# Weights of plain blocks and output units: hi and lo split in two parts of 1024 columns instead of four of 512

## The chip, the cores and the metric

The kernel runs on one core of one Trainium2 chip. The metric is device time in microseconds (us) for one call, the median of the runs. Engines are named as in the profile: PE (matrix multiply), DVE (vector), ACT (scalar), POOL (the third elementwise engine), SP (the queue that issues the transfers).

## The reference

One step of a hybrid layer on 512 new prompt tokens and 8 sequences of 8 sample tokens, all float32, D_MODEL 2048. The layer normalises x, projects it, runs a gated linear attention branch (GLA, 4 heads) and a gated delta branch (GDN, 16 heads, with a causal convolution of width 4 on q, k and v), projects both, merges them through sigmoid gates and projects once more. Cut to its core:

```python
h = _rmsnorm(x, ln_g)
proj = h @ w_in
o_a, s_gla_new = _gla_chunked(q_a, k_a, v_a, log_alpha, s_gla)
y_a = (_rmsnorm(o_a, gla_norm_g) * silu(gate_a)) @ w_br_a
qkv, conv_new = _causal_conv(qkv_b, conv_buf, conv_w)
o_b, s_gdn_new = _gdn_chunked(q_b, k_b, v_b, g, beta, s_gdn)
y_b = (_rmsnorm(o_b, gdn_norm_g) * silu(gate_b)) @ w_br_b
out = x + (sigmoid(m_a) * y_a + sigmoid(m_b) * y_b) @ w_out
```

The result is the final norm of `out` and the new states of both branches and of the convolution, for prompt and sample.

## The kernel before

The 576 tokens (512 prompt, 64 sample) are the moving side of nearly all matrix products. A **block** is 128 columns of a weight matrix, all 2048 rows deep: in SBUF a tile of 128 partitions by 16 k-steps by 128 columns, 2048 elements in a partition. `load_raw` (one SP transfer of 1024 KB) brings it in as `raw`. `split` makes two tiles from it: `hi`, the weights cast to fp32r, on ACT (line 249, ACT CAST hi), and `lo = raw - hi`, on DVE (line 252; on POOL for the blocks 0 and 2). Each k-step of `run_half` then issues three products, hi by the first and the second part of the tokens and lo by the first, for 256 tokens (half 0) and again for 320 (half 1). `raw`, `hi` and `lo` have two buffers each, so block i+1 is split while block i is multiplied.

`split` has four parts (`NSPL`), each a quarter of the columns: 512 elements a partition. Part j of block i+1 is written in `run_half` of block i, two in each half (after k-steps 1 and 9). The same holds, with other counters, for the output units (`run_unit`) and for the last group before them. The two branch projections (`run_pairs`) have their own `pairs_prep`, which casts and subtracts in pieces of 1024 already (lines 383 and 384); `split` only calls it.

Beside the blocks run many **side tasks**, written as generators (`key_task`, `query_task`, `value_task`, `vtask`, `gla_chain`, `solve` and others). `S.pump`, called after each k-step, resumes those whose due time has come; the clock `S.t` counts the estimated time of PE instructions alone. PE's order is fixed by that: `manual_schedule` holds for PE. ACT, DVE, POOL and SP are put in order by the framework's scheduler, from the order of writing and its own estimates. Each engine runs its row strictly in order.

Names that come up below:

- GLA values: `vT<-mm` (line 1274) copies each half of a value block from PSUM on ACT; then `vtask` transposes it on PE (`vtp`, line 125) and casts it (`vth`, line 1229). There are 4 such blocks in each of 4 heads.
- GDN queries and values: ACT scales (`acc`, line 859), DVE adds three taps of the convolution (`acc`, line 861); per chunk of a head DVE computes `z` (line 1428), PE multiplies `np_<-z,U`, DVE copies `nn` (line 1434), PE multiplies `spd<-nn,ke`.
- `conv_rows` (line 872): PE transposes `lp`, DVE copies it out as `ls` (line 879), PE transposes `lpp` into the same ring of three PSUM buffers. `vh`, `vhs` and `U` are DVE copies of the next head's values and of its solved triangle (lines 1406, 1408, 1349).
- Decay of GLA: DVE adds a bias to `lg` and gets `ab` (line 798), a chain over four rows j on DVE and POOL (`scb` and `ab`, lines 813 to 818) ends in one transfer `d_c<-ab` a row (line 821). The second group of four rows reuses the tile `ab`, so its first `ab` waits for the last `d_c`.
- `key_task`: SP loads `R<-d_gh` (line 941, one buffer), POOL adds a mask to it (lines 943 and 945), ACT makes `W` from it (lines 948 and 950).

Of the kernel before, what the change touches and what calls it, by code (L numbers as in the profile page):

```python
# [103 lines left out]
def build(ctx, tc, nc, x_p, x_s, st_gla, st_gdn, st_conv, ln_g, w_in, w_al, b_al, conv_w,  # L104
# [76 lines left out]
    blocks = []  # L181
# [33 lines left out]
            SY.dma_start(raw, b["wd"][:, c0:c0 + P].rearrange("(k p) c -> p k c", p=P))  # L215
        wts[i] = [raw, None, None]

    NSPL = 4

    NM0, NMP, NMG, NMD, NM1 = 5, 0, 3, 3, 12  # L220

    def split(i, j, eng=V):

        if i >= len(blocks):
            return
        if blocks[i]["wd"] is None:
            if j in (1, 3):
                pairs_prep(blocks[i], j // 2)  # L230
            return
        w = wts[i]
        narrow = blocks[i]["col"] is None
        if i == len(blocks) - 1:
            if j == 0:
                w[1:] = (ost["pr"].tile([P, KT, P], F32R, name=n) for n in ("hi_", "lo_"))
        elif j == 0 and narrow:
            w[1] = p0c.tile([P, KT, 112], F32R, name="hin")
            G.memset(w[1][:, :, 48:64].bitcast(F32), 0.0)
        elif j == 0:  # L240
            w[1] = wp.tile([P, KT, P], F32R, name="hi", tag="whi")
            w[2] = wp.tile([P, KT, P], F32R, name="lo", tag="wlo")
        raw, hi, lo = w
        s = slice(j * KT // NSPL, (j + 1) * KT // NSPL)
        if narrow:
            raw, hi, lo = raw[:, s], hi[:, s, 0:48], hi[:, s, 64:112]
        else:
            raw, hi, lo = raw[:, s], hi[:, s], lo[:, s]
        hc = A.copy(hi, raw)  # L249
        if i > 2:  # L250
            S.marks[A] = hc
        cut = eng.tensor_tensor(out=lo, in0=raw, in1=hi.bitcast(F32), op=ALU.subtract)  # L252
        if eng is V:
            last_split[0] = cut
# [3 lines left out]
    def run_half(i, hf, ps):  # L258
        b = blocks[i]
        rh, rl = b["rhs"]  # L260
        narrow = b["col"] is None
        m = 112 if narrow else P
        _, hi, lo = wts[i]
        t0, t1 = HALVES[hf]
        out = ps[0:m, 0:t1 - t0]
        for k in range(KT):
            r1, r2 = rh(k)[:, t0:t1], rl(k)[:, t0:t1]
            mm(out, hi[:, k, 0:m], r1, start=(k == 0), stop=False)
            mm(out, hi[:, k, 0:m], r2, start=False, stop=(narrow and k == KT - 1))
            if not narrow:  # L270
                mm(out, lo[:, k, 0:m], r1, start=False, stop=(k == KT - 1))
            if i >= 3 and k % 8 == 1:
                split(i + 1, hf * 2 + k // 8)
            elif i == 2 and hf == 1 and k % 4 == 1:
                split(3, k // 4)
            S.pump()
        b["evac"](hf, out, slice(t0, t1))

# [118 lines left out]
    def run_pairs(i):  # L397
        b = blocks[i]
        cols = b["pairs"]
        n = len(cols)  # L400
        t1, t2 = slice(0, TH), slice(TH, T)
        for p in range(n):
# [3 lines left out]
            for j in range(7):  # L406
                g = 7 * p + j
# [12 lines left out]
                for kk in range(KH):  # L420
# [4 lines left out]
                    if kk == 1:  # L425
# [9 lines left out]
                            pairs_raw(b, p + 1, 0)  # L435
                        elif j == 3:
                            pairs_raw(b, p + 1, 1)
                    if g == 7 * n - 1 and kk % 2 == 0:
                        if kk == 0:
                            pr_.pop(("hi", 0)), pr_.pop(("lo", 0))  # L440
                        split(i + 1, kk // 2)
                    S.pump()
                for kk in range(KH):
                    r1, r2 = b["rhs"](j, kk)
# [63 lines left out]
    def run_unit(i):  # L508

        b = blocks[i]  # L510
        g, q = b["col"]
# [5 lines left out]
        end_ = len(blocks) - 1  # L517
# [4 lines left out]
        for n, (u, j, c) in enumerate(order):  # L522
            hi, lo = (x.rearrange("p (j a) c -> p j (a c)", j=4)[:, j] for x in wts[u][1:])
            k = blocks[u]["col"][1] * 4 + j
# [7 lines left out]
            else:  # L532
                both = [(accs[c], m[:, TP:TP + P], hi), (accs[c][0:TS], m[:, T:T + TS], lo)]
                for out, w, x in both[::-1] if last else both:
                    mm(out, w, x, start=(first and x is hi), stop=(last and x is hi))
            if n % 5 == 1 and i < end_ - 1:
                split(i + 1, n // 5)
            if n % 5 == 3 and i == end_ - 2:
                split(i + 2, n // 5)
            S.pump()  # L540
            if last:
                b["evac"](g, c, accs[c])
# [1569 lines left out]
    def third():  # L2112
        for j in range(NSPL):
            split(2, j, G)
# [37 lines left out]
```

## Time and profile before

| what | value |
| --- | --- |
| median of 3 runs | 2812.85 us (2811.58 to 2815.17) |
| profiled execution, its own time | 2812.57 us |
| its span | 2810.9 us |
| PE busy | 2763.3 us, 98% of the span |
| DVE busy | 1804.4 us, 64% |
| ACT busy | 1103.3 us, 39% |
| POOL busy | 364.7 us, 13% |
| mean granted PE clock | 0.994 |

The clock that the throttle grants PE stands at full speed in all 40 slices of the page. PE is idle for 2810.9 - 2763.3 = 47.6 us in all. An engine's time counts for the kernel's time only where PE waits for it, so the list of PE's waits and the slack of its other operands are what to read.

### The profile page before, as it was taken

To read this page: it belongs to the slowest core of one execution; us is meant where nothing else is said; L and a number is where in the kernel's file an instruction comes from. 1 tells how busy PE (TensorE), PEld (TensorE's weight loads), DVE (VectorE), ACT (ScalarE), POOL (GpSimd) and SP (SyncE) were. 2 spreads that over 40 slices of the span, in tenths; PEclk is the share of its full clock that TensorE was granted. 3 is DMA by queue.
4 is the path that set the end of the run, shared out by engine and by line. 5 is a ranking of instruction groups with operands and counts; after the bars stand their busy time and mean duration, and the time that the engine had idled before them with its cause. 6 is when DMAs were issued, how large, how long until landed. Compare 5 with 4: busy or idle time off the path is not lost.

```text
span 2810.9 us, 49996 instructions
## 1 busy us (share of the span) xinstructions
PE 2763.3 (98%) x19726; PEld 2630.9 (94%) x19726; DVE 1804.4 (64%) x3456; ACT 1103.3 (39%) x2449; POOL 364.7 (13%) x545
## 2 busy tenths in 40 slices
PE   8999999999999999999999999999989999999998
PEld 7999999999999999999999999999879889999776
DVE  7767765765567888734666666647754667877333
ACT  5444445565423232223333333336643334434222
POOL 2000000442101010101222222212210010000111
PEclk9999999999999999999999999999999999999999
DMA  5333335565652333435444444457766988657522
GB/s 164 121 120 116 122 118 151 153 182 173 169 128 79 109 96 91 145 90 156 126 122 124 125 120 122 130 146 199 226 220 215 300 285 270 197 175 242 175 76 97
DMA packets 546281, 433.97 MB, mean 154 GB/s; under 512 B 75125, under 2 KB 468293, under 8 KB 544117
## 3 DMA queue, kind: packets, MB, share of 16 engines
q1 hardware_dynamic: 546046, 430.78, 50.7%
q8 instruction: 155, 2.54, 0.4%
q14 instruction: 80, 0.66, 0.1%
HBM read 322.69 MB, written 108.00 MB: 153 GB/s over the span
## 4 chain that ended last, share of the span: by engine, by line
PE 89%; DVE 4%; DMA 1%; ACT 1%; POOL 1%; issue 1%; SPq 0%; DVEq 0%; POOLq 0%; ACTq 0%
PE mm L115 71%; PE oacc L115 7%; PE opd L115 1%; PE sps L115 1%; DVE tmp L906 1%; PE sp L115 1%; DMA raw<-in_w_br_a 1%; PE ksq L115 1%; PE spd L115 1%; PE qk L115 1%; DVE lo L252 0%; PE ksp L115 0%; PE kk L115 0%; DVE nt L909 0%; PE op L125 0%
## 5 line engine op out<-in xcount | busy, mean ns | idle before, releaser
L115 PE MATMUL mm<-hh,hi 128*128 128x256 f32 (+2 forms) x3968 | 1194.6, 304 | 0.0
L115 PE MATMUL mm<-hl,hi 128*128 128x256 f32 (+2 forms) x3968 | 1161.6, 295 | 0.0
L115 PE MATMUL mm<-hh,lo 128*128 128x256 f32 (+2 forms) x3968 | 1117.0, 295 | 0.8 <-DVE lo L252 0.8
L115 PEld LDWEIGHTS mm<-hh,hi 128*128 128x128 f32 x3968 | 748.5, 189 | 10.1 <-issue 4.5
L115 PEld LDWEIGHTS mm<-hl,hi 128*128 128x128 f32 x3968 | 748.9, 189 | 2.1
L115 PEld LDWEIGHTS mm<-hh,lo 128*128 128x128 f32 x3968 | 729.2, 188 | 1.3 <-DVE lo L252 1.0
L252 DVE TENSOR_TENSOR lo<-raw,hi 128x512 fp32r<-128x512 f32 x568 | 398.6, 720 | 315.4 <-ACT hi L249 307.2
L249 ACT CAST hi<-raw 128x512 fp32r<-128x512 f32 x572 | 329.6, 619 | 485.4 <-PE mm L115 407.8
L115 PE MATMUL mm<-lb,hi 128*128 128x320 f32 (+1 forms) x1024 | 208.1, 298 | 0.0
L115 PE MATMUL oacc<-hi,m 128*128 128x512 f32 x540 | 174.1, 395 | 0.0
L115 PEld LDWEIGHTS mm<-lb,hi 128*128 128x128 f32 x1024 | 163.7, 188 | 9.5 <-issue 7.8
L383 ACT CAST hi<-raw 128x1024 fp32r<-128x1024 f32 x96 | 100.9, 1051 | 182.1 <-PE mm L115 105.4
L384 DVE TENSOR_TENSOR lo<-raw,hi 128x1024 fp32r<-128x1024 f32 x96 | 117.3, 1222 | 77.1 <-ACT hi L383 75.3
L115 PE MATMUL mm<-lb,lo 128*128 128x320 f32 (+1 forms) x512 | 150.7, 294 | 0.0
L115 PE MATMUL mm<-tl,hi 128*128 128x288 f32 x512 | 137.7, 295 | 0.0
L115 PE MATMUL mm<-th,hi 128*128 128x288 f32 x512 | 137.6, 296 | 0.0
L906 DVE TENSOR_TENSOR tmp<-nt 128x1 f32<-128x1 f32 (+36 forms) x163 | 131.6, 807 | 3.0
L115 PEld LDWEIGHTS oacc<-hi,m 128*128 128x128 f32 x540 | 101.1, 188 | 28.0 <-DVE mth L462 0.4
L861 DVE SCALAR_TENSOR_TENSOR acc<-ext,cwT,acc 128x600 f32<-128x600 f32 x144 | 120.2, 835 | 0.8 <-ACT acc L859 0.6
L115 PE MATMUL oacc<-lo,m 128*128 128x512 f32 x300 | 118.1, 395 | 0.0
L383 ACT CAST hi<-s 128x1024 fp32r<-128x1024 f32 x72 | 74.8, 1047 | 105.3 <-DVE s L371 50.2
L1449 ACT COPY od<-opd 128x128 f32<-128x128 f32 x64 | 16.8, 262 | 242.2 <-PE opd L115 242.2
(891 smaller groups left out, 3993.1 us busy)
## 6 DMA issues: line engine op xcount, KB each, us to landing
raw<-in_w_in SPq DMA_DIRECT2D x144, 1024.0 KB
raw<-in_w_br_b SPq DMA_DIRECT2D x16, 1024.0 KB
Sb<-in_state_gla SPq DMA_DIRECT2D x32, 512.0 KB
out<-Sb SPq DMA_DIRECT2D x32, 512.0 KB
raw<-in_w_br_a SPq DMA_DIRECT2D x16, 1024.0 KB
raw<-in_w_out SPq DMA_DIRECT2D x16, 1024.0 KB
Sbd<-in_state_gdn SPq DMA_DIRECT2D x16, 512.0 KB
out<-Sbd SPq DMA_DIRECT2D x16, 512.0 KB
```

The costliest lines, as they stand in the source:

```text
L115: PE.matmul(out, lhsT, rhs, start=start, stop=stop, **kw)
L249: hc = A.copy(hi, raw)
L252: cut = eng.tensor_tensor(out=lo, in0=raw, in1=hi.bitcast(F32), op=ALU.subtract)
L383: S.marks[A] = A.copy(hi, src)
L384: last_split[0] = V.tensor_tensor(out=lo, in0=src, in1=hi.bitcast(F32), op=ALU.subtract)
L861: V.scalar_tensor_tensor(out=acc, in0=ext[:, i:i + 600], scalar=cw(i), in1=acc, op0=ALU.mult, op1=ALU.add)
L906: V.tensor_tensor(out=tv, in0=nt[:, cs, c0:i], op=ALU.mult, in1=nt[:, c0:i, i:i + 1].rearrange("p j o -> p o j").broadcast_to([P, m, i - c0]))
L1449: A.copy(o_[:, c], op_[:, 0:P])
```

## The change

`NSPL` is 2: a part is half of the columns, 1024 elements a partition. The calls are thinned out to match: in `run_half` one part in each half, after k-step 1 (it was k-steps 1 and 9), in block 2 both parts in its second half, in the last pair group at kk 0 and 4, in the units at n 1 and 11 (n 3 and 13 for the unit after next). `pairs_prep` is called with j directly, so both its calls come at k-step 1 of a half instead of k-step 9. Computation, tiles, buffers and transfers are the same.

```diff
-    NSPL = 4
+    NSPL = 2
...
         if blocks[i]["wd"] is None:
-            if j in (1, 3):
-                pairs_prep(blocks[i], j // 2)
+            pairs_prep(blocks[i], j)
             return
...
-            if i >= 3 and k % 8 == 1:
-                split(i + 1, hf * 2 + k // 8)
-            elif i == 2 and hf == 1 and k % 4 == 1:
-                split(3, k // 4)
+            if i >= 3 and k == 1:
+                split(i + 1, hf)
+            elif i == 2 and hf == 1 and k % 8 == 1:
+                split(3, k // 8)
...
-                    if g == 7 * n - 1 and kk % 2 == 0:
+                    if g == 7 * n - 1 and kk % 4 == 0:
                         if kk == 0:
                             pr_.pop(("hi", 0)), pr_.pop(("lo", 0))
-                        split(i + 1, kk // 2)
+                        split(i + 1, kk // 4)
...
-            if n % 5 == 1 and i < end_ - 1:
-                split(i + 1, n // 5)
-            if n % 5 == 3 and i == end_ - 2:
-                split(i + 2, n // 5)
+            if n % 10 == 1 and i < end_ - 1:
+                split(i + 1, n // 10)
+            if n % 10 == 3 and i == end_ - 2:
+                split(i + 2, n // 10)
```

PE's row is the same instruction for instruction. DVE's row goes from 2790 to 2566 entries, ACT's from 1643 to 1570, and the scheduler puts the side tasks' instructions in other places among the splits. Line numbers from 230 on are one lower in the changed kernel. Three places follow.

The first is the decay chain of GLA's first group. POOL before, the rows j = 2 and 3 of the chain; `sqk` and `R` belong to two `key_task`s:

```order
L814 COPY scb<-ab 128x4
L815 COPY scb<-ab 128x4
L816 COPY scb<-ab 128x8
L818 TENSOR_TENSOR ab<-ab,scb 128x512
L968 TENSOR_TENSOR sqk<-tb,halfc 128x5
L943 TENSOR_TENSOR R<-R,maskb 128x512
L814 COPY scb<-ab 128x4
L815 COPY scb<-ab 128x4
L816 COPY scb<-ab 128x8
L945 TENSOR_TENSOR R<-R,maskb 128x64
L818 TENSOR_TENSOR ab<-ab,scb 128x512
```

POOL now, at the start of the chain (row j = 0 begins with L813):

```order
L843 MEMSET ext 128x3
L846 COPY ext<-hisk 128x8x3
L942 TENSOR_TENSOR R<-R,maskb 128x512
L944 TENSOR_TENSOR R<-R,maskb 128x64
L813 COPY scb<-ab 128x4
L814 COPY scb<-ab 128x4
L815 COPY scb<-ab 128x8
L817 TENSOR_TENSOR ab<-ab,scb 128x512
```

SP before, the same place; the load of this `R` stands behind two `d_c`:

```order
L821 DMA d_c_105<-ab 128x576
L215 DMA raw<-in_w_in 128x16x128
L821 DMA d_c_106<-ab 128x576
L941 DMA R<-d_gh 128x576
L821 DMA d_c_107<-ab 128x576
L991 DMA d_W_180<-W 128x512
L992 DMA d_W_180<-W 64x64
L821 DMA d_c_108<-ab 128x576
```

SP now:

```order
L990 DMA d_W_180<-W 128x512
L940 DMA R<-d_gh 128x576
L991 DMA d_W_180<-W 64x64
L215 DMA raw<-in_w_in 128x16x128
L820 DMA d_c_105<-ab 128x576
L820 DMA d_c_106<-ab 128x576
```

The two additions to `R` moved from the end of the chain to before its start, and the load of `R` from behind the second `d_c` to behind the preceding head's `W`.

The second place is a value block of GLA, on ACT (`hi` is the next block's first cast). Before:

```order
L1274 COPY vT<-mm 128x256
L249 CAST hi<-raw 128x512
L1274 COPY vT<-mm 128x320
L249 CAST hi<-raw 128x512 x2
L1229 CAST vth<-vtp 128x4x128
```

Now:

```order
L1273 COPY vT<-mm 128x256
L248 CAST hi<-raw 128x1024
L1273 COPY vT<-mm 128x320
L248 CAST hi<-raw 128x1024
L1228 CAST vth<-vtp 128x4x128
```

The order is the same; what stands between the two copies of `vT` is one cast of 1024 instead of one of 512.

The third place is the delta stage, DVE. First the start of a query block, before:

```order
L1465 TENSOR_TENSOR oT<-op_18634,gtd 128x512
L252 TENSOR_TENSOR lo<-raw,hi 128x512
L1428 SCALAR_TENSOR_TENSOR z<-ksp_18675,neghc,vh 128x128
L861 SCALAR_TENSOR_TENSOR acc<-ext,cwT,acc 128x600
L252 TENSOR_TENSOR lo<-raw,hi 128x512
```

Now:

```order
L1464 TENSOR_TENSOR oT<-op_18298,gtd 128x512
L251 TENSOR_TENSOR lo<-raw,hi 128x1024
L860 SCALAR_TENSOR_TENSOR acc<-ext,cwT,acc 128x600
L1427 SCALAR_TENSOR_TENSOR z<-ksp_18339,neghc,vh 128x128
L860 SCALAR_TENSOR_TENSOR acc<-ext,cwT,acc 128x600
```

A tap of the convolution now stands ahead of `z`, and the `lo` ahead of both is the long one; this pattern stands in six heads. Then `conv_rows` at the end of a group of four heads, before:

```order
L886 COPY lp<-lpp 12x128
L1406 TENSOR_SCALAR vh<-vp,sqk 128x128 x3
L879 COPY ls<-lp 96x128
L1406 TENSOR_SCALAR vh<-vp,sqk 128x128
L1408 TENSOR_SCALAR vhs<-vps,sqk 64x128
L1349 TENSOR_SCALAR U_17558<-up 64x4x64
```

Now:

```order
L885 COPY lp<-lpp 12x128
L1405 TENSOR_SCALAR vh<-vp,sqk 128x128 x4
L1407 TENSOR_SCALAR vhs<-vps,sqk 64x128
L1348 TENSOR_SCALAR U_17242<-up 64x4x64
L878 COPY ls<-lp 96x128
```

The second `ls` moved behind the last `vh`, `vhs` and `U`; this stands at three places of the stage.

## Rows read from the trace of the kernel before

**Rows 1.** The page, busy time of each engine over the span.

```profile
PE 2763.3 (98%) x19726; PEld 2630.9 (94%) x19726; DVE 1804.4 (64%) x3456; ACT 1103.3 (39%) x2449; POOL 364.7 (13%) x545
```

**Rows 2.** PE's waits over the whole span: us in total, times, longest.

```profile
PE ksp L125 <- issue: 13.4, 1, 13.4
PE lg L115 <- DVE ab L798: 3.5, 1, 3.5
PE mm L115 <- DVE lo L252: 0.8, 1, 0.8
```

**Rows 3.** The page, costliest groups: busy us, mean ns | idle before, releaser.

```profile
L252 DVE TENSOR_TENSOR lo<-raw,hi 128x512 fp32r<-128x512 f32 x568 | 398.6, 720 | 315.4 <-ACT hi L249 307.2
L249 ACT CAST hi<-raw 128x512 fp32r<-128x512 f32 x572 | 329.6, 619 | 485.4 <-PE mm L115 407.8
...
L383 ACT CAST hi<-raw 128x1024 fp32r<-128x1024 f32 x96 | 100.9, 1051 | 182.1 <-PE mm L115 105.4
L384 DVE TENSOR_TENSOR lo<-raw,hi 128x1024 fp32r<-128x1024 f32 x96 | 117.3, 1222 | 77.1 <-ACT hi L383 75.3
```

**Rows 4.** Timeline, ACT and PE, one value block: start us, us, idle in brackets.

```profile
833.30 0.62 ACT L249 CAST hi<-raw 128x512 fp32r<-128x512 f32 x1 [6.53 <-PE mm L115]
833.83 0.42 ACT L1274 COPY vT<-mm 128x320 f32<-128x320 f32 x1
...
834.32 0.71 PE L125 MATMUL vtp<-ident,vT 128*128 128x128 f32 x5
```

**Rows 5.** Timeline, DVE and PE, `conv_rows` at one of its three places.

```profile
1572.19 0.28 DVE L879 COPY ls<-lp 96x128 f32<-96x128 f32 x1
...
1572.90 0.41 DVE L1349 TENSOR_SCALAR U<-up 64x256 f32<-64x256 f32 x1
...
1572.52 0.28 PE L125 MATMUL lpp<-ident,lvP 128*12 128x128 f32 x1 [0.44 <-DVE ls L879]
```

**Rows 6.** Timeline, ACT, DVE and PE, start of a query block, one of six.

```profile
1646.11 0.63 ACT L249 CAST hi<-raw 128x512 fp32r<-128x512 f32 x1
...
1646.77 0.69 DVE L252 TENSOR_TENSOR lo<-raw,hi 128x512 fp32r<-128x512 f32 x1
1647.38 0.34 DVE L1428 SCALAR_TENSOR_TENSOR z<-ksp,neghc,vh 128x128 f32<-128x128 f32 x1
...
1649.24 0.38 PE L115 MATMUL np__18697<-z,U 128*128 128x128 f32 x2
```

**Rows 7.** Timeline, DVE and PE, another block's start, one of fourteen alike.

```profile
1613.80 0.69 DVE L252 TENSOR_TENSOR lo<-raw,hi 128x512 fp32r<-128x512 f32 x1 [1.56 <-ACT hi L249]
1614.49 0.84 DVE L861 SCALAR_TENSOR_TENSOR acc<-ext,cwT,acc 128x600 f32<-128x600 f32 x1
1615.26 0.35 DVE L1428 SCALAR_TENSOR_TENSOR z<-ksp,neghc,vh 128x128 f32<-128x128 f32 x1
...
1616.55 0.39 PE L115 MATMUL np__18284<-z,U 128*128 128x128 f32 x2
```

**Rows 8.** Timeline, ACT, SP and POOL, the decay chain and the loads of `R`.

```profile
504.73 0.37 SPq L941 DMA_DIRECT2D R<-d_gh  x1
...
508.87 1.28 POOL L943 TENSOR_TENSOR R<-R,maskb 128x512 f32<-128x512 f32 x1 [2.67 <-DMA R<-d_gh]
...
525.82 0.50 POOL L814 COPY scb<-ab 128x4 f32<-128x4 f32 x1 [2.32 <-DVE ab L813]
...
525.87 0.33 ACT L950 ACTIVATE W<-R,nghc 64x64 f32<-64x64 f32 x1
...
543.25 0.32 SPq L821 DMA_DIRECT2D d_c<-ab  x1
```

**Rows 9.** Timeline, POOL, `lo` of block 2 in the startup.

```profile
30.50 3.05 POOL L252 TENSOR_TENSOR lo<-raw,hi 128x512 fp32r<-128x512 f32 x2 [1.91 <-ACT hi L249]
```

**Rows 10.** Timeline, DVE and SP, a raw load of `w_br_a`.

```profile
2396.74 1.29 DVE L252 TENSOR_TENSOR lo<-raw,hi 128x512 fp32r<-128x512 f32 x2
...
2399.17 0.43 SPq L341 DMA_DIRECT2D raw<-in_w_br_a  x1
```

## The prediction

> **What bounds the kernel now.** The page comes first: PE is busy 2763.3 of 2810.9 us, DVE 1804.4, ACT 1103.3 [rows 1]. So PE sets the time, and a shorter cast or subtraction is worth nothing in itself; what counts is where PE waits, 47.6 us in all. The list of PE's waits is read next. It names a `lo` once, for 0.8 us [rows 2]: that is all that the splits cost now. The other large waits have other causes: 13.4 us for a transfer, 3.5 us for the decay chain `ab` [rows 2]. Last come the timelines where a side task's result reaches PE with little to spare, because there a longer split, or one in another place, makes a new wait. I looked for every operand of PE that is ready less than about 1 us before its use, and asked the two orders what now stands ahead of its producer.
>
> **What the split saves, and why it is off the path.** A `lo` of 512 takes 720 ns, one of 1024 takes 1222; a `hi` of 512 takes 619, one of 1024 takes 1051 [rows 3] (the long rows are those of the pair blocks, the same operations on the same tiles). A block needs 4 x 720 = 2880 ns of DVE before and 2 x 1222 = 2444 now, and 2476 against 2102 of ACT. For 568/4 = 142 blocks that is 62 us of DVE and 53 us of ACT. All of it lies beside PE: DVE sits idle for 315.4 us ahead of its `lo`s, waiting for ACT, and ACT for 485.4 us ahead of its `hi`s, mostly waiting for PE to let go of a buffer [rows 3]. Taken as nothing. What it costs: whoever stands behind a part now waits for 1051 ns of ACT or 1222 of DVE instead of 619 or 720.
>
> **GLA value blocks, +3.2 us.** The cast starts when PE frees the buffer, at 833.30; the second copy of `vT` follows it at 833.83, 0.53 later, and ends at 834.25 [rows 4]. PE's five transposes start at 834.32, 0.11 apart; the third is the first that reads the second copy, near 834.54, so the copy has 0.29 to spare [rows 4]. With the long cast the copy starts 1.051 - 0.619 = 0.43 later. A result that PE waits for is used some 0.05 us after it is there (the `ls` of rows 5: ready 1572.47, used 1572.52), so 0.24 is really spare, and PE waits about 0.20. ACT was idle for 6.53 us before [rows 4], so nothing else shifts that. Sixteen blocks (four in each of four heads): 16 x 0.20 = 3.2 us. Bounds: 0, if PE gets there that much later itself, and 16 x 0.43 = 6.9, if nothing is spare. I take 3.2, worked from the block's own rows.
>
> The Trainium skill has a sentence against this change (Perfetto Trace Analysis, Optimizing Scalar/DVE Operations): where these engines are not saturated but make bubbles elsewhere, breaking instructions up may help. The same section says that grouping pays if the engine is saturated. By the second rule the sum would be a gain, at most the 47.6 us that PE stands idle; by the first a loss, as worked out here from the rows. At 64% and 39% busy the trace sides with the first.
>
> **`conv_rows`, +2.5 us.** PE's `lpp` waits for the second `ls` already: ready 1572.47, used 1572.52 [rows 5]. Now `ls` stands behind the fourth `vh`, `vhs` and `U`. The work is the same, only permuted, so `ls` ends when `U` did, at 1572.90 + 0.41 = 1573.31, and `lpp` starts about 0.84 later. Three places: 2.5 us. Behind `lpp` PE has only its own row, nothing there gives the time back. Lower bound 0, if PE comes later itself; upper 3 x 1.2, if a `lo` gets in between.
>
> **`z` in the delta stage, +1.3 us (0 to 6).** At the start of six query blocks `z` follows the first `lo` directly and ends at 1647.72, 1.52 before PE's use at 1649.24 [rows 6]. Now the long cast ends at 1646.11 + 1.05 = 1647.16, 0.39 later than the old `lo` began; the `lo` is 0.50 longer; and a tap of the convolution goes ahead, 0.77 from its start to the next [rows 7]. Together 1.66 against 1.52 - 0.05: PE waits 0.2, six times 1.2 to 1.3. In fourteen other starts the order stays, `lo`, tap, `z`, and `z` ends 0.94 before its use [rows 7]; there the delay is 0.39 + 0.50 = 0.89 against 0.94 - 0.05: it comes out even. That is the thinnest margin of the sum. If each of the twenty lost 0.3, it would be 6. The first head and the copies near it add about 0.4, by the same durations.
>
> **The decay chain, +2.3 us (-1.5 to +4.4).** PE stands 3.5 us for `ab` [rows 2], which waits for the last `d_c`, issued at 543.25 by a chain on POOL that runs from 525.82 without a gap to speak of [rows 8]. Two changes meet there. POOL's two additions to `R` leave the chain: about 1.28 + 0.3 us less [rows 8]. But they now stand ahead of its first operation, and `R` can only be loaded when the last `W` of the preceding head is read. That ended at 526.2 [rows 8]; ACT has some 2 us less ahead of it now (two casts fewer, and `W` goes before the other activations), so about 524. From issue to use the load took 508.87 - 504.73 = 4.14 us [rows 8]. POOL then adds until about 529.7, and the chain starts 3.9 later and is 1.6 shorter: +2.3. If the load came as early as 520 it would be -1.5; if `W` came no earlier than before, +4.4. The four `d_c` themselves are moved past nothing that waits longer than POOL does.
>
> **Startup, +0.7 (0 to 1.6).** POOL subtracts two parts of block 2 in 3.05 us [rows 9]; PE takes the first as soon as it is there. One piece of 1024 is ready some 1.5 us later than one of 512. Two later waits of PE in the startup depend on DVE, not on PE's pace, and take half of it back.
>
> **Block 4, -0.8 us.** The one wait for a `lo` [rows 2] goes: DVE now makes both parts ahead of other work that it had taken first. What is late next there is nothing that the trace shows.
>
> **Raw buffer of `w_br_a`, -1.1 us.** Its load was issued at 2399.17, though the last `lo` had read the buffer at 2398.03 [rows 10]: SP had other transfers ahead. Now it stands first, and later waits of PE for DVE hang on that load. Bounds -1.5 and 0.
>
> **The sum.** 3.2 + 2.5 + 1.3 + 0.4 + 2.3 + 0.7 - 0.8 - 1.1 = +8.5 us. Against the profiled execution's own 2812.57 that is 2821.1; the median lies 0.28 above that execution, so 2821.3.
>
> **The rivals.** *No change that can be measured* (chance 0.27). PE is late by itself at these places, so that one wait swallows the next, and the load of `R` comes early enough. For it: all margins are tenths of a microsecond, and the trace's own rows differ by that. Then the GLA blocks give 1, `conv_rows` 2.5, the chain 0, the rest 0: about 2816. It decides at the copy of `vT`: below 0.24 of extra cast PE loses nothing.
>
> *Faster* (chance 0.06). The gap of 13.4 us [rows 2] is a wait for a transfer queued behind others. If the raw loads, whose buffers come free earlier, had drained the queues by then, it would go, and with half of the added waits the time would be 2812.9 + 4.2 - 13.4 = 2804. Against it: SP's order at that gap is the same as before, and what the queue waits for there is a state that PE's own pace makes ready.
>
> *Much slower* (chance 0.17). The fourteen `z` that come out even fall behind by 0.3, and `R` comes late: 4.2 + 2.1 = 6.3 us more, 2827.6, and with as much again from the copies `nn` behind each `z` some 2832. It decides at the first tenth by which a block's `lo` is longer than the row says [rows 7].
>
> **How the numbers follow.** The forecast, 2815 to 2827, gets 0.5, and its point is 2821.3. The range reaches into the rivals on both sides, 2811 to 2829; outside I leave the faster case and the upper half of the much slower one, together about 0.2. About 0.2%, 5.6 us, is what a measurement of this kernel can tell from no change. Below 2807.2: 0.06. From there to 2818.5: no change, 0.27, and the lower end of the forecast, 0.08, so 0.35. Above: 0.42 of the forecast and 0.17, so 0.59.
>
> **What would show it.** PE's waits after should name `vT` or `vtp` sixteen times with 0.2 us, `lpp` with three times 1.2 instead of 0.4, `z` six times, `ab` with 5 to 6 us, and no `lo`. DVE's busy time should fall by about 60 us and ACT's by about 50, PE's should not move. If PE's waits are the same and DVE's busy time has fallen, the first rival holds; if the 13.4 us have shrunk, the second.

## The result and the profile after

The changed kernel takes 2835.26 us (median of 4 runs, 2834.20 to 2837.19) against 2813.18 us for the kernel before (4 runs, 2811.58 to 2815.17) beside it: a ratio of 1.0083, with a 95% interval of 1.0072 to 1.0095. It is 22 us slower. The prediction had slower as the likeliest sign, at 2821.3 us, but the range ended at 2829.

The page of the changed kernel, busy time of each engine and the two groups of the split (busy us, mean ns | idle before, releaser), to be read against [rows 1, 3]:

```profile
span 2832.5 us, 49400 instructions
...
PE 2770.8 (98%) x19726; PEld 2635.0 (93%) x19726; DVE 1778.0 (63%) x3170; ACT 1073.1 (38%) x2159; POOL 379.8 (13%) x541
...
L251 DVE TENSOR_TENSOR lo<-raw,hi 128x1024 fp32r<-128x1024 f32 x284 | 353.3, 1250 | 325.4 <-ACT hi L248 322.8
L248 ACT CAST hi<-raw 128x1024 fp32r<-128x1024 f32 x286 | 296.4, 1049 | 487.4 <-PE mm L115 406.8
```

DVE and ACT have less to do, by 26 and 30 us in all. PE's idle time has grown from 47.6 to 61.7 us and its busy time by 7.5, with the same instructions. PE's waits (us in total, times, longest) name where, against [rows 2]:

```profile
PE ksp L125 <- issue: 13.5, 1, 13.5
PE mm L115 <- DVE qd L1250: 6.6, 1, 6.6
PE kp L125 <- DVE kT L864: 4.5, 1, 4.5
...
PE lg L115 <- DVE ab L797: 2.5, 1, 2.5
...
PE lpp L125 <- DVE vhs L1407: 2.3, 3, 0.8
...
PE mm L115 <- POOL lo L251: 1.3, 1, 1.3
```

The first line is the old one, unchanged. The next two are one stop each: that for `qd` is new, that for `kT` was 0.81 us at the same place before. Neither `qd` nor `kT` was in the sum. `ab` has become shorter, not longer.

PE runs the same 19726 instructions in the same order in all the kernels of this study, so the shift of one instruction against the kernel before can be followed through the run. The table is worked out from the traces: by how many us PE fell behind the kernel before in each stretch (minus: got ahead; the stretches are times of the kernel before). It has one profiled execution of each kernel. Stretches that a kernel leaves as they were differ by up to 1.1 us before 620, by 0.3 between 620 and 1900 and by up to 1.5 behind that; less than this means nothing.

| kernel | to 500 | 500-580 | 580-620 | 620-810 | GLA 810-1300 | delta 1300-1900 | to the end |
|---|---|---|---|---|---|---|---|
| after | -0.7 | -1.8 | +5.1 | +9.9 | +4.1 | +6.1 | -1.4 |
| e1 four, early | -1.3 | +2.5 | +0.4 | -0.1 | +0.8 | +8.8 | -0.5 |
| e2 two `ls` | -0.6 | -0.4 | +5.0 | +1.6 | +4.2 | +3.0 | -1.1 |
| e3 all `W` behind `th` | -0.9 | +5.1 | +0.5 | +14.3 | +4.2 | +5.9 | -1.0 |
| e4 e3, two `ls` | -0.5 | +3.7 | +1.5 | +8.4 | +4.3 | +3.1 | -0.8 |
| e5 one `W` group | -0.4 | -0.3 | +2.4 | +9.9 | +4.2 | +5.0 | -0.5 |
| e6 key stage only | +0.6 | -2.0 | +3.6 | +10.1 | -0.1 | 0.0 | +0.9 |
| e7 GLA only | +1.0 | +1.1 | -0.1 | -0.1 | +4.3 | -0.1 | +0.7 |
| e8 delta only | -0.2 | +0.1 | -0.9 | 0.0 | 0.0 | +5.7 | -1.5 |
| e9 `hi` 2, `lo` 4 | -1.1 | -4.4 | +0.6 | +0.8 | +4.4 | +6.4 | +0.5 |
| e10 `hi` 4, `lo` 2 | +0.2 | -0.4 | +3.7 | +1.6 | +1.1 | +16.1 | +3.7 |
| e11 late | +4.1 | -0.4 | -0.8 | +9.6 | +6.9 | +6.3 | -0.8 |
| e12 before, two `ls` | 0.0 | 0.0 | -0.1 | +0.8 | 0.0 | -1.5 | +0.9 |
| e13 key stage as e9 | -0.6 | -3.7 | +0.7 | +1.0 | -0.3 | 0.0 | -0.4 |
| e14 e13, two `ls` | -0.8 | -3.5 | +0.6 | +0.8 | -0.3 | -1.5 | +0.4 |

Fifteen of the 22 us are lost in two stretches of the key stage, nearly all of it at two stops and just behind them (1.3 us are an `lpp` at 768 that waits for the second `ls`).

**The stop at 592.** Timelines of the changed kernel, ACT, DVE, POOL and PE (start us, us, idle in brackets):

```profile
590.04 0.40 ACT L947 ACTIVATE W<-R,nghc 128x128 f32<-128x128 f32 x1 [5.03 <-POOL R L942]
590.34 0.35 ACT L844 COPY ext<-mm 128x256 f32<-128x256 f32 x1
590.60 0.70 ACT L863 ACTIVATE th<-acc 128x600 f32<-128x600 f32 x1
...
591.33 0.69 DVE L864 SCALAR_TENSOR_TENSOR kT<-th,acc 128x512 f32<-128x512 f32 x1 [3.20 <-ACT th L863]
...
588.74 1.26 POOL L942 TENSOR_TENSOR R<-R,maskb 128x512 f32<-128x512 f32 x1 [5.82 <-DMA R<-d_gh]
...
592.08 1.11 PE L125 MATMUL kp<-ident,kT 128*128 128x128 f32 x4 [4.54 <-DVE kT L864]
```

And the same place in the kernel before:

```profile
589.39 0.71 ACT L864 ACTIVATE th<-acc 128x600 f32<-128x600 f32 x1 [2.64 <-DVE acc L861]
...
593.08 1.28 ACT L948 ACTIVATE W<-R,nghc 128x128 f32<-128x128 f32 x4 [2.72 <-POOL R L943]
```

Read from the end: PE's `kp` waited 4.54 us for `kT`, `kT` for `th`, and `th` (ready to go since the last `acc` at 588.1) stood on ACT behind a `W` that waited 5.03 us for POOL's addition to `R`, that for a transfer. From 588.1 to its start at 590.60 are 2.5 of the 4.54 us. In the kernel before `th` is ahead of that `W`. ACT, which goes through its row in order, passed a wait for a DMA on to a short operation that PE needed.

**The stop at 798.** The changed kernel, DVE, SP and ACT:

```profile
768.86 0.29 DVE L878 COPY ls<-lp 96x128 f32<-96x128 f32 x1 [4.52 <-DMA out<-ls]
...
779.59 0.29 DVE L878 COPY ls<-lp 96x128 f32<-96x128 f32 x1 [2.65 <-DMA out<-ls]
787.16 2.36 DVE L251 TENSOR_TENSOR lo<-raw,hi 128x1024 fp32r<-128x1024 f32 x2 [7.28 <-ACT hi L248]
789.89 0.28 DVE L878 COPY ls<-lp 96x128 f32<-96x128 f32 x1
797.97 0.82 DVE L1250 SCALAR_TENSOR_TENSOR qd<-mm,ec 128x256 f32<-128x256 f32 x2 [6.90 <-ACT ec L1247]
...
790.20 0.67 SPq L880 DMA_DIRECT2D out<-ls  x1
790.97 0.41 SPq L215 DMA_DIRECT2D raw<-in_w_in  x1
792.99 0.34 SPq L1245 DMA_DIRECT2D cb<-d_c  x1
...
797.26 0.68 ACT L1247 ACTIVATE ec<-cb 128x576 f32<-128x576 f32 x1 [9.19 <-DMA gtc<-d_ga]
```

The kernel before, DVE, SP and ACT:

```profile
767.90 0.29 DVE L879 COPY ls<-lp 96x128 f32<-96x128 f32 x1 [1.91 <-DMA out<-ls]
...
775.40 0.29 DVE L879 COPY ls<-lp 96x128 f32<-96x128 f32 x1 [2.49 <-DMA out<-ls]
...
782.38 0.33 SPq L1246 DMA_DIRECT2D cb<-d_c  x1
...
786.72 0.69 ACT L1248 ACTIVATE ec<-cb 128x576 f32<-128x576 f32 x1 [2.29 <-DVE tmp L906]
```

`ls` has one buffer here, so each copy waits until the transfer of the one before has read it; they come 4 to 11 us apart. Before, the last was done at 775.7. After, the last but one comes only at 779.59, and the last then stands behind the next block's two `lo` until 789.89. SP issues in order: the output row, a raw load, and then `cb`, 10.6 us later than before (792.99 against 782.38). `ec` needs `cb`: the row names the transfer `gtc` behind it, but `ec` starts 4.3 us after the issue of `cb` in both kernels (797.26 and 786.72). `qd` needs `ec`, and `qd` is what frees the PSUM buffer that PE wants at 798.

**The clock behind the stops.** Stretches of the changed kernel (start:end, length, busy us of PE, PEld, DVE, ACT and POOL with counts, granted clock, DMA share, GB/s), and then the first stretch of the kernel before:

```profile
546.00:560.00 14.00, 14.00 (x110) 13.81 (x109) 13.01 (x29) 5.11 (x8) 3.67 (x7) 1.00 0.64 197
592.00:606.00 14.00, 13.92 (x88) 13.67 (x89) 9.12 (x21) 7.20 (x24) 4.83 (x7) 0.79 0.52 159
792.00:806.00 14.00, 7.54 (x38) 7.55 (x39) 1.15 (x3) 1.36 (x2) 0.35 (x2) 0.76 0.38 117
```

```profile
546.00:560.00 14.00, 13.92 (x95) 13.58 (x96) 12.04 (x31) 5.28 (x10) 3.88 (x7) 0.88 0.67 216
```

Right after PE had stood for 4.5 us the mean granted clock of 14 us was 0.79, so part of the stretch ran at the lower level (1.2 instead of 2.4 GHz), and PE lost a further 2.7 us until 600 (its shift grew from 1.20 to 3.86) while it was busy throughout. After the 6.6 us it was 0.76, and 1.9 us more were lost. The kernel before has one such place, behind its 3.5 us for `ab`, with 0.88; the changed kernel with its 2.5 us there shows 1.00. (The page's digits for the clock of the kernel before are 9 in all 40 slices, that is 90% or more of 70 us each, not full speed throughout.) By the stretches of the table PE's busy time grew by 2.5 and 2.2 us around these two stops, by 3.0 in GLA (the steps at `vtp` below count as busy) and by 3.0 in the delta stage, and fell by 3.2 in the other three: 7.5 in all.

### The profile page after: what moved, and what is told of

Its sections match the earlier page's. It is cut to its first block, busy times and chain, and to the rows that moved or that the text cites. A ratio compares the mean times of both kernels' runs of the same rounds, so it can differ in the third digit from the quotient of the medians.

```text
span 2832.5 us, 49400 instructions
## 1 busy us (share of the span) xinstructions
PE 2770.8 (98%) x19726; PEld 2635.0 (93%) x19726; DVE 1778.0 (63%) x3170; ACT 1073.1 (38%) x2159; POOL 379.8 (13%) x541
## 5 line engine op out<-in xcount | busy, mean ns | idle before, releaser
L251 DVE TENSOR_TENSOR lo<-raw,hi 128x1024 fp32r<-128x1024 f32 x284 | 353.3, 1250 | 325.4 <-ACT hi L248 322.8
L248 ACT CAST hi<-raw 128x1024 fp32r<-128x1024 f32 x286 | 296.4, 1049 | 487.4 <-PE mm L115 406.8
L382 ACT CAST hi<-raw 128x1024 fp32r<-128x1024 f32 x96 | 100.9, 1051 | 176.7 <-PE mm L115 96.0
L383 DVE TENSOR_TENSOR lo<-raw,hi 128x1024 fp32r<-128x1024 f32 x96 | 117.2, 1221 | 69.7 <-ACT hi L382 69.2
```

Of the source, the lines that this page charges most:

```text
L382: S.marks[A] = A.copy(hi, src)
L383: last_split[0] = V.tensor_tensor(out=lo, in0=src, in1=hi.bitcast(F32), op=ALU.subtract)
```

## The experiments

The theory after the two traces: a part of 1024 is a longer piece in the queues of ACT and DVE, so it delays what stands behind it and lets the scheduler put side tasks in another order; the two long stops are orders of that kind. The first rival: it is the place where the parts are written (all at the head of a half), not their length. The second: the stops have other causes, and the orders are not to blame.

**e1: four parts at the places of two.**

```diff
-    NSPL = 2
+    NSPL = 4
...
             if i >= 3 and k == 1:
-                split(i + 1, hf)
+                split(i + 1, 2 * hf)
+                split(i + 1, 2 * hf + 1)
```

> The changed kernel, but each half of a block is again split in two parts of 512 columns, which are written together at the place in the program where the changed kernel writes its one part of 1024. Length theory: it is the length of the pieces that cost (a piece of 1024 that cannot be interrupted makes GLA's vT copies wait, and lets the scheduler put the first W ahead of th on ACT and the fourth ls behind the next block's lo on DVE). It expects the order of before to come back at those two places, the stops of 4.5 us at kp (592) and 6.6 us at mm <- qd (798) to be gone, no 0.19 us stops at vtp, and 2809 to 2819 us. Place theory: it is where the splits are written, all at the head of a half instead of spread through it. It expects both stops and about 2835 us. A time between, 2823 to 2830, would say that both count.

Measured: 2823.07 us, ratio 1.0035 (1.0023 to 1.0048). Both stops and all stops at `vtp` are gone; up to 1300 us of the run this kernel is 2.2 us behind the kernel before, the changed one 16.6. But it waits 5.7 us for `ab` at 546, and the delta stage costs 8.8 us: there fourteen starts of a block wait 0.47 us for `z`, and one 0.86. DVE at one of them:

```profile
1620.30 0.69 DVE L252 TENSOR_TENSOR lo<-raw,hi 128x512 fp32r<-128x512 f32 x1 [1.56 <-ACT hi L249]
1620.99 0.84 DVE L866 SCALAR_TENSOR_TENSOR acc<-ext,cwT,acc 128x600 f32<-128x600 f32 x1
1621.75 0.68 DVE L252 TENSOR_TENSOR lo<-raw,hi 128x512 fp32r<-128x512 f32 x1
1622.35 0.84 DVE L866 SCALAR_TENSOR_TENSOR acc<-ext,cwT,acc 128x600 f32<-128x600 f32 x1
1623.11 0.35 DVE L1433 SCALAR_TENSOR_TENSOR z<-ksp,neghc,vh 128x128 f32<-128x128 f32 x1
```

Against [rows 7], one `lo` and one tap more stand ahead of `z`. So length counts for the two long stops and for GLA, and place for the delta stage: neither alone. The time between the two forecasts was the case left for that, and 2823 is at its edge.

**e2: a second buffer for `ls`.**

```diff
-            ls = pl.tile([96, P], F32, name="ls", tag="ls", bufs=1)
+            ls = pl.tile([96, P], F32, name="ls", tag="ls", bufs=2)
```

> The changed kernel with two buffers instead of one for ls in conv_rows, so that the third and fourth ls need not wait until the output transfers of the first and second have read theirs. Theory: SP holds the load of the next raw and the load cb <- d_c behind the late fourth output row, and the qd of the query stage waits for that load; it expects cb to start some 7 us earlier, the stop of 6.6 us at mm <- qd near 798 gone, the slow clock after it (worth about 1.9 us) gone too, and 2825 to 2828 us. Rival: the fourth ls stays behind the block's two long lo on DVE whatever buffers it has (it is put there by the scheduler, not by the buffer), or qd is late for another reason; then the time stays at 2835 us.

Measured: 2825.09 us, ratio 1.0046 (1.0033 to 1.0059), within the theory's bounds. The stretch of 620 to 810 falls from +9.9 to +1.6. SP issues `cb` at 788.04, 5 us earlier rather than 7, and PE still waits 1.5 us for `qd`; the clock of 792 to 806 is 1.00. The three `lpp` of the delta stage gain too, which was not foreseen. The chain from `ls` over SP to PE is shown. PE's wait in e2:

```profile
PE mm L115 <- DVE qd L1250: 1.5, 1, 1.5
```

**e3 and e4: `W` behind `th` everywhere, without and with e2.**

```diff
-            A.activation(W[:, c * P:(c + 1) * P], R[:, c * P:(c + 1) * P], AF.Exp,
-                         bias=nghc[:, c, h:h + 1])
+            with tc.issue_after(last_th[0].ins):
+                A.activation(W[:, c * P:(c + 1) * P], R[:, c * P:(c + 1) * P], AF.Exp,
+                             bias=nghc[:, c, h:h + 1])
```

> The changed kernel with the copy W of the decay chain held on ACT until the last th of the key stage has been issued, the order of before. Theory: th stands behind W, which waits for R, and kT, kp and TensorE wait for th; it expects the stop of 4.5 us at kp (592) gone, and the granted clock from 592 to 606 back from 0.79 to about 1.0 (2.4 us), of which 1.25 us comes back as the stop at 606 that the changed kernel no longer has: 2829 to 2831 us. Rival: with th early the W is late and the chain of 606 to 640 is what waits: 2835 us or more, with the stop moved to after 606.

> Both edits of the two kernels before this one (W behind th on ACT, two buffers for ls). If the two stops are apart, the gains add: 2819 to 2823 us, 6 to 10 us above the kernel before, which would be what GLA's vT copies (3.2 us), the z of the gated delta blocks (1.7), conv_rows (1.0) and the up matmuls (1.7) cost together. If one of them only uncovers the other, less than 10 us is gained against the changed kernel.

Measured: 2842.20 us (1.0104, 1.0090 to 1.0118) and 2832.78 (1.0074, 1.0060 to 1.0088). The theory's numbers failed for both. The stretch of 580 to 620 did fall from +5.1 to +0.5, but the `W` of other heads were late now, and the stretches around it lost 7 us more at 500 to 580 and 4 at 620 to 810 (new waits of up to 3.7 us at `kp` and `lg`). The edit was too wide to test the one place. The two together differ from e3 by 9.4 us, as e2 does from the changed kernel by 10.2: in the times that gain adds, though at 620 to 810 it is 5.9 us here and 8.3 there.

**e5: one group of `W` alone.**

```diff
+        with tc.issue_after(last_th[-2].ins) if h == 5 else ExitStack():
             for c in range(4):
                 A.activation(W[:, c * P:(c + 1) * P], R[:, c * P:(c + 1) * P], AF.Exp,
                              bias=nghc[:, c, h:h + 1])
             A.activation(W[0:TS, TP:T], R[0:TS, TP:T], AF.Exp, bias=nghc[0:TS, 4, h:h + 1])
```

> The changed kernel with one thing moved: at the one key block of 592 us the five W of the decay task stand behind th on ACT instead of ahead of it; every other instruction of every engine stands where it stood. (The run that held all W behind th also moved the W of eight other blocks, and lost there what it gained here.) Theory: the stop of 4.5 us at kp <- kT and the slow clock behind it come from th waiting behind W for R; both go, the stop at 606 of about 1.2 us comes back, 2829 to 2831 us. Rival: kT is late for another reason (acc, the lo of 1024 on DVE), and the time stays at 2835 us.

Measured: 2833.27 us, ratio 1.0070 (1.0056 to 1.0084). The median is 2 us below that of the changed kernel, where 4 to 6 were expected, and the two intervals overlap, so the time alone does not show the gain. The trace does, as half of what was expected: 580 to 620 costs 2.4 us instead of 5.1, and `kp` waits 2.9 instead of 4.5. Timeline, DVE, POOL and ACT:

```profile
590.78 1.51 DVE L866 SCALAR_TENSOR_TENSOR kT<-th,acc 128x512 f32<-128x512 f32 x1 [0.77 <-ACT th L865]
...
590.48 1.26 POOL L944 TENSOR_TENSOR R<-R,maskb 128x512 f32<-128x512 f32 x1 [5.68 <-DMA R<-d_gh]
...
583.30 0.23 ACT L827 ACTIVATE g_em<-scb 128x32 f32<-128x32 f32 x1 [7.35 <-POOL scb L813]
583.72 0.35 ACT L847 COPY ext<-mm 128x256 f32<-128x256 f32 x1
...
590.04 0.70 ACT L865 ACTIVATE th<-acc 128x600 f32<-128x600 f32 x1 [2.89 <-DVE acc L862]
```

`th` is ahead of `W` now but starts at 590.04, because there is a second wait of the same kind: the copies `ext`, from which `acc` is made, stand behind `g_em`, which waits for POOL's chain (in the kernel before they run at 579.08, ahead of it). And `kT` took 1.51 us instead of 0.69, while POOL added to `R`. So the order of `W` and `th` is a cause of the stop, worth about half. The other two are read from the rows; no run removed them.

**e6, e7, e8: one stage at a time.** The kernel before, with two parts only for the blocks of one stage (e7: 32 to 62, e8: 63 to 97):

```diff
     NSPL = 4
+    nspl = lambda i: 2 if 8 <= i < 32 else 4
...
-            if i >= 3 and k % 8 == 1:
+            if i >= 3 and nspl(i + 1) == 2:
+                if k == 1:
+                    split(i + 1, hf)
+            elif i >= 3 and k % 8 == 1:
                 split(i + 1, hf * 2 + k // 8)
```

> The kernel before with the change in the key stage alone: blocks 8 to 31 in two parts of 1024, all others in four of 512 at their old places. From the traces of the changed kernel the key stage costs 0.7 to -1.5 at the decay chain, 4.8 at 592, 1.3 at 769 and 8.6 at 798. Theory: these belong to the key stage alone and do not hang on what was changed ahead of it: 2824 to 2829 us. Rival: one of the two long stops is a coincidence of offsets that come from the start of the kernel: then only one of them is there and the time is 2816 to 2822.

> The kernel before with the change in the GLA stage alone: blocks 32 to 62 in two parts, all others in four. Theory: the long hi on ACT stands ahead of vT and costs 16 times 0.19 us, and with the waits for ath about 4.1 us in all: 2816.5 to 2818.5 us. Rival: the stage has slack that the offset from the key stage took away, and alone it costs less than 1.5 us: up to 2815.

> The kernel before with the change in the gated delta stage alone: blocks 63 to 97 in two parts, all others in four. The changed kernel lost 6.1 us there: seven z of 0.25, three lpp of 0.32, 1.7 at three up matmuls, the rest small. Theory: these come from the two-part blocks of this stage: 2818 to 2820 us. Rival: the waits of the up matmuls for U and vh are coincidences of the offset, and only z and lpp are left: 2815.5 to 2817. The three stages should add up with what is outside of them (about -1.5 us) to the 22 us of the whole change.

Measured: 2827.22 us (1.0050, 1.0037 to 1.0062), 2818.37 (1.0017, 1.0009 to 1.0026) and 2818.23 (1.0018, 1.0009 to 1.0027), all within their theory. That is 14.1, 5.2 and 5.1 us above the 2813.16 of the kernel before in that series, 24.4 in all against the 22 of the whole change. In the table each loses in its own stage what the changed kernel loses there, and elsewhere no more than unchanged stretches differ by (for 580 to 620 it is 3.6 instead of 5.1). The stops belong to their stages, not to an offset from the start.

**e9 and e10: `hi` and `lo` apart.** The changed kernel with each `lo` cut in two (e9), or each `hi` (e10, likewise):

```diff
         hc = A.copy(hi, raw)
...
-        cut = eng.tensor_tensor(out=lo, in0=raw, in1=hi.bitcast(F32), op=ALU.subtract)
+        for q in range(2):
+            e = slice(q * KT // 4, (q + 1) * KT // 4)
+            cut = eng.tensor_tensor(out=lo[:, e], in0=raw[:, e], in1=hi[:, e].bitcast(F32),
+                                    op=ALU.subtract)
```

> The changed kernel with only the hi copies (ACT) in parts of 1024; each lo subtraction (DVE) is two of 512 written one after the other. In this program the five W of the 592 block stand behind th again, while the fourth ls of the key stage still stands behind two halves' lo. Theory (the stop at 592 comes from W ahead of th, the one at 798 from ls behind lo, the 16 vT stops from the long hi): stop at 592 at most 1.5 us, stop at 798 of 6 to 7 us, vtp stops of 0.2 still there; in the gated delta stage lo, acc, lo, acc stand ahead of z as in the first run, some 8 us: 2829 to 2835 us. Rival (lo's length is what costs, ACT has room): about 2818 us.

> The mirror image: only the lo subtractions in parts of 1024, each hi copy two of 512 written one after the other. In this program one W of the 592 block stands ahead of th, and the third and fourth ls of the key stage stand ahead of the next block's lo. Theory: stop at 592 of 3 to 4.5 us with a slow clock behind it, no stop at 798, no vtp stops of 0.2 (hi can be interrupted at 512), about 5 us lost in the gated delta stage: 2820 to 2825 us. Rival (hi's length is what costs): about 2814 us.

Measured: 2819.71 us (1.0027, 1.0017 to 1.0037) and 2836.41 (1.0082, 1.0069 to 1.0096). Both forecasts failed, and taught most.

At `vtp` the two come apart as the theory said: sixteen steps of 0.19 us, 3.1 in all, in every kernel with `hi` of 1024 in GLA (after, e2 to e5, e7, e9, e11), and none in those with 512 (e1, e10 and the others).

At 798 neither has the long stop: 0.8 and 1.6 us. The fourth `ls` of e9, which the order showed behind four `lo`, stands behind those of the block before, and comes at 770.98 already. The long stop is there only in kernels with both parts long. At 592 e10 has it (4.5 us) and e9 does not, as expected.

In the delta stage e10 loses 16 us: fourteen `z` of 1.00 us. DVE at one:

```profile
1627.81 0.84 DVE L862 SCALAR_TENSOR_TENSOR acc<-ext,cwT,acc 128x600 f32<-128x600 f32 x1 [2.25 <-ACT acc L860]
1628.57 1.22 DVE L253 TENSOR_TENSOR lo<-raw,hi 128x1024 fp32r<-128x1024 f32 x1
1629.70 0.84 DVE L862 SCALAR_TENSOR_TENSOR acc<-ext,cwT,acc 128x600 f32<-128x600 f32 x1
1630.45 0.34 DVE L1429 SCALAR_TENSOR_TENSOR z<-ksp,neghc,vh 128x128 f32<-128x128 f32 x1
```

The `lo` of 1024 has to wait for its second `hi`, a tap goes first, and `z` is behind all of it.

And e9 is 4.4 us *ahead* of the kernel before at 500 to 580, where the forecast had nothing. Its POOL adds to `R` at 539.22, behind the whole decay chain; the kernel before does it in the chain's middle (538.87, with the last link at 542.19), the changed kernel ahead of it (527.12, with the first link at 529.22). No run moved this addition alone, so that its place is the cause is argued from the rows.

**e11: the two parts later in each half.**

```diff
-            if i >= 3 and k == 1:
+            if i >= 3 and k == 9:
```

> The changed kernel with its two parts written at the tenth k of a half instead of the second, so some 5 us later in each half, past the copies of the half before. In this program W stands behind th at 592, and the fourth ls of the key stage still stands behind the lo. Theory: no long stop at 592, the stop at 798 stays (6 to 7 us and about 1.9 us of slow clock), no vtp stops since hi is no longer issued next to vT, and z of the gated delta stage no longer has lo ahead of it: 2820 to 2826 us. Rival: the splits, ready only late in the half before their use, make TensorE wait for lo at block starts: above 2830 us, with mm <- lo among its waits.

Measured: 2838.99 us, ratio 1.0095 (1.0081 to 1.0109): a miss by 13 us at the least. The stop at 592 is short (1.1 us) and the one at 798 stays (6.7), as expected; so for the stop at 592 the place counts as well as the length. But the sixteen steps at `vtp` are there, since a `hi` that is written later still starts when PE frees its buffer; the delta stage is no better; the `lo` of blocks 2 and 4 cost 1.8 and 2.4 us at the start; and GLA has new waits at `oTp` and `ath`. The rival had this time (above 2830) and this wait for `lo`, but it makes 4 of the 25 us. Of the two places that were tried, none is good for a part of 1024.

**e12: e2's edit on the kernel before.**

> The kernel before with two buffers for ls in conv_rows and nothing else. Theory: the three stops of 0.60 us at lpp <- ls go, 1.8 us: 2811 to 2812 us. Rival: vhs or lp is next late there, less than 0.6 us is gained and the time is that of the kernel before, 2813 us.

Measured: 2810.65 us, ratio 0.9998 (0.9990 to 1.0007). In the trace the three `lpp` gain 0.51 each, 1.5 us, and 0.8 is lost at 798. No difference that can be measured.

**e13 and e14: the key stage with long `hi` alone.** The kernel before, with e9's form in blocks 4, 5 and 8 to 31; e14 adds two buffers for `ls` in the delta stage alone.

```diff
+    nspl = lambda i: 2 if 4 <= i < 32 and i not in (6, 7) else 4
...
+        for q in range(4 // nspl(i)):
+            e = slice(q * KT // 4, (q + 1) * KT // 4)
+            cut = eng.tensor_tensor(out=lo[:, e], in0=raw[:, e], in1=hi[:, e].bitcast(F32),
+                                    op=ALU.subtract)
```

> The kernel before, with hi copies of 1024 and lo subtractions of 512 written at the head of a half in blocks 4, 5 and 8 to 31 alone; all other blocks as before. In this program R's add stands behind the last d_c of the first decay group on POOL, W behind th at 592. Theory (the place of R's add sets the stop at 546): the stop there is under 1 us, no slow clock behind it, 4 to 5 us less than before until 800 and nothing after that: 2808 to 2810 us. Rival: the gain of that kernel came from offsets, and the time is that of before, 2812 to 2815 us.

> The kernel before this one, and two buffers for ls in the conv_rows of the gated delta stage alone (in the run with two buffers everywhere three waits at lpp shrank by 0.51 us each, and the key stage lost 0.8). If the gains add, 2806.5 to 2808.5 us, 1.5 us below the kernel before this one; if not, the same time as that.

Measured: 2810.07 us (0.9991, 0.9982 to 1.0000) and 2809.45 (0.9986, 0.9977 to 0.9995). Both lie above what was expected (2808 to 2810, and 2806.5 to 2808.5), and e14 is 0.6 us below e13 instead of 1.5, which can't be told from nothing. Their traces gain 3.7 and 3.5 us at 500 to 580 and little elsewhere, except e14's 1.5 at `lpp`. POOL and SP of e13, and its stretch behind the stop:

```profile
539.76 2.52 POOL L950 TENSOR_TENSOR R<-R,maskb 128x512 f32<-128x512 f32 x1
...
537.29 2.86 SPq L828 DMA_DIRECT2D d_c<-ab  x2
...
546.00:560.00 14.00, 14.00 (x107) 13.93 (x108) 12.09 (x29) 6.26 (x17) 7.70 (x7) 1.00 0.64 195
```

The chain's last `d_c` leaves some 3 us earlier than in [rows 8], the wait for `ab` is 1.3 instead of 3.5 (under 1 was expected), and the clock behind it stays at 1.00 instead of 0.88. The gain is the stage's own. e14 is faster than both kernels, than the one before by 0.14%; e13's interval touches no change.

## Why the prediction was wrong

**What bounds the kernel, and the saving at nothing:** right. PE's time set everything. The `lo` group fell by 45 us and the `hi` group by 33, and none of it came back as time. The 62 and 53 of the prediction multiply means of records that overlap; from the busy sums in [rows 3] it is 398.6 - 284 x 1.222 = 52 and 329.6 - 286 x 1.051 = 29. Of its signs, DVE fell by 26 us in all instead of about 60, ACT by 30 instead of about 50, and PE's busy time, which should not move, rose by 7.5. Nothing of the sum hangs on these.

**GLA value blocks, +3.2:** right in mechanism and size. Sixteen steps of 0.19 us make 3.1. The changed kernel, ACT and PE, as in [rows 4]:

```profile
845.70 1.05 ACT L248 CAST hi<-raw 128x1024 fp32r<-128x1024 f32 x1 [6.52 <-PE mm L115]
846.65 0.41 ACT L1273 COPY vT<-mm 128x320 f32<-128x320 f32 x1
...
846.71 0.96 PE L125 MATMUL vtp<-ident,vT 128*128 128x128 f32 x5
```

The copy starts 0.95 after the cast instead of 0.53, and the five transposes last 0.96 instead of 0.71. The stage lost 1.1 more, most of it at `ath`, which the sum did not have.

By the section of the Trainium skill that the prediction weighed (Perfetto Trace Analysis, Optimizing Scalar/DVE Operations), breaking instructions up may help where ACT and DVE are not saturated but cause bubbles; the sixteen steps fit this, and the gain that grouping can bring to a saturated engine did not come.

**Delta stage, 2.5 + 1.3 + 0.4 = +4.2:** the stage lost 6.1 (5.7 alone, in e8). `z` has seven stops of 0.25, 1.7 us, and the thin margin of the fourteen others held. `lpp` was sized too large: 0.32 three times, not 0.84. The second `ls` is not what it waits for now: at 1591.88 `lpp` starts 1.36 us ahead of that `ls`, and its releaser is `vhs`, done at 1591.82, ahead of `U` (1592.16). Three `up` matmuls that now wait 0.5 to 0.7 us for `U` or `vh`, 1.7 us, were missing; the rest is in steps too small to name.

**The decay chain, +2.3:** the sign was wrong, -1.8 in its stretch (and -2.0 in e6). The start of the chain was foreseen within half a us (529.22 against 529.7), but the chain's length was taken as the old one less 1.6. It ran only to about 541.9, since its own links were shorter than in the kernel before (12.7 us in all, where 17.4 - 1.6 = 15.8 was assumed), so the wait for `ab` fell by 1.0; and the clock behind it stayed at 1.00, which gave about 1.2 more and for which the sum had no term. The lower bound, -1.5, was passed. In e9, e13 and e14, with `R` behind the chain, the stretch gained 3.5 to 4.4.

**Startup, block 4 and `w_br_a`:** -1.2 in the sum, -2.1 in the trace. Block 4 was right: PE's step there fell by 0.97 in every kernel of the table that changes this block and in none that leaves it as it was (e6, e7, e8, e12). The other two can't be judged. PE's step at block 2 grew by 1.43, but by 1.12 in e7, which leaves it as it was, and the 1.25 gained at 2421 are gained in e8 as well.

**The terms together:** outside the two long stops the trace has +6.3 us, against the +8.5 of the sum. That this is so close is in part luck: the decay chain came out 4.1 lower than its term and the startup and end 0.9 lower, the delta stage 1.9 and GLA 0.9 higher.

**The step that failed** is the search itself, in the first part: "every operand of PE that is ready less than about 1 us before its use", and "what now stands ahead of its producer". Both long stops passed through it. `kT` met the first test: PE's waits in the kernel before name it, 0.81 us at the place that became the stop at 592. `qd`, which frees a buffer, had as little to spare: PE's product started 0.48 after the start of `qd`, and 0.49 in the changed kernel (798.46 against 797.97), so in both it started as soon as it could. Wait list and timelines of the kernel before, DVE and PE:

```profile
PE kp L125 <- DVE kT L865: 1.9, 2, 1.1
...
787.44 0.82 DVE L1251 SCALAR_TENSOR_TENSOR qd<-mm,ec 128x256 f32<-128x256 f32 x2 [0.56 <-ACT ec L1248]
...
787.92 0.41 PE L115 MATMUL mm<-hh,hi 128*128 128x320 f32 x1
```

And the second test looked one producer back, on its own engine. `kT` and `qd` stand two and four steps behind the operations that moved: `W` ahead of `th` on ACT, then `kT` on DVE; `ls` behind `lo` on DVE, then SP's queue, `cb`, `ec`, `qd`. What SP holds behind an output row was not followed. The two stretches are 15 us, of which 4.6 are the clock behind the stops, for which the prediction had no term. The much slower rival ended near the measured time, but by the fourteen `z`, which did not move; that it came near is luck.

## What to carry to other kernels

Where a scheduler orders the engines, a change of a piece's length is a change of order everywhere: go through the order for each wait on a DMA that has come ahead of something short (here `W` ahead of `th`), and for each copy into a single buffer that feeds an in-order queue, and follow both to PE, however many engines that takes. Start from the waits and thin margins that are there already, however small: both long stops grew out of one. Price a stop of PE with the clock behind it, not by its length alone. And cut the two halves of a split separately, by engine and by stage: long `hi` with short `lo` put the key stage some 3 us ahead in the traces of e13 and e14 (0.1% of the time, at the edge of what was measured), long `hi` alone cost 16 x 0.19 us in GLA, and long `lo` behind short `hi` cost 14 x 1.0 in the delta stage.

## What the runs showed of the hardware

The granted clock after a stop did not follow its length alone. Behind waits of 4.5 and 6.6 us it was 0.79 and 0.76 over 14 us, but 0.88 behind the 4.5 us of e10. Behind a wait of 2.5 us for `ab` it was 1.00 in the changed kernel, but 0.89 in e5, with the same 2.5 us. These two executions of the same instructions in that stretch differ by some 1.5 us, most of it by the clock.

An addition on POOL and `kT` or `lo` on DVE did not run side by side at full speed. In e5 POOL's addition to `R` began at 590.48 and took 1.26 us, as where DVE is idle (588.74 in the changed kernel); `kT`, begun at 590.78, took 1.51 instead of 0.69 and ended 0.55 behind it. In e13 `kT` began at 539.73, ahead of POOL's addition at 539.76, and DVE went through `kT`, its second part and a `lo` at their usual lengths. POOL's addition took 2.52 and ended 1.13 behind that `lo`:

```profile
540.47 0.68 DVE L255 TENSOR_TENSOR lo<-raw,hi 128x512 fp32r<-128x512 f32 x1
```

In the kernel before, the addition at 538.87 took 1.29 beside DVE's `ke` and `N`, which read PSUM. So the length of a chain on one of the two hangs on what the other has at that moment.

The Trainium skill (Trainium Architecture — The Big Picture, What this means for kernel authors) says that these two engines contend at a pair of ports that they share, under an exclusive lock, not by splitting the bandwidth. The rows of e5 and e13 agree: the one that waited added nearly a whole length of its own (0.55 of 0.69, 1.13 of 1.26) behind the other's end.
